# A hybrid encoder block on one core: residual with tokens on the partitions, down and output projections with activations as stationary operand

## The chip, the cores and the metric

The kernel runs on one core of one Trainium2 chip. A core has a matrix engine (TensorE, PE in the profile; PEld is its weight load), a vector engine (VectorE, DVE), a scalar engine (ScalarE, ACT), a general engine (GpSimd, POOL) and an engine that issues transfers (SyncE, SP). TensorE multiplies a stationary operand of up to 128 x 128 with a moving operand of up to 512 columns and adds into PSUM, a memory of eight banks of 512 float32 for each of 128 partitions. The metric is the device time of one execution in microseconds, as the median of the runs.

## The reference

One block of an encoder on 512 tokens of 1024 features, all in float32: a half feed-forward layer, a token mixer of two branches, a second half feed-forward layer, a norm. The projections dominate.

```python
def rms_norm(x, g):
    return x * rsqrt(mean(x * x, axis=-1) + 1e-6) * g

def swiglu_ffn(h, w_gate, w_up, w_down):          # hidden width 2816
    return (silu(h @ w_gate) * (h @ w_up)) @ w_down

x = x + 0.5 * swiglu_ffn(rms_norm(x, ffn1_norm), ffn1_w_gate, ffn1_w_up, ffn1_w_down)
h = rms_norm(x, mix_norm)
u_a, v_a, q_r, k_r, v_r, g_r, gate_a, gate_b = split(h @ w_in + b_in)      # eight times 1024 columns
a = spatial_gating(gelu(u_a), gelu(v_a), ...)                              # 128-position chunks
r = bidirectional_retention(rotary(q), rotary(k) / 16, v, decay)           # four heads of 256
r = r * rsqrt(mean(r * r, per head) + 1e-6) * silu(g_r)
mix = sigmoid(gate_a) * (a @ w_branch_a) + sigmoid(gate_b) * (r @ w_branch_b)
x = x + mix @ w_out
x = x + 0.5 * swiglu_ffn(rms_norm(x, ffn2_norm), ffn2_w_gate, ffn2_w_up, ffn2_w_down)
return rms_norm(x, final_norm)
```

## The kernel before

Every float32 product is made of three matmuls (`mm3`, lines 90 to 93): each operand is split into a part hi that a single pass carries exactly and the rest lo, and hi·hi, hi·lo and lo·hi are added up in PSUM. Weights come in tiles of 1 MB (`load_w`, lines 80 to 88): SyncE loads `raw`, ScalarE copies it to `whi` (line 85), VectorE subtracts to `wlo` (line 87). Each of the three kinds has two buffers. Activations are split in the same way into tiles of the pool `act` with 60 buffers; PSUM is a ring of eight banks.

The residual x lies with features on the partitions: x[m] holds 128 features of all 512 tokens. A projection (`proj`, line 95) has 128 columns of a weight as the stationary operand and 512 tokens as the moving one, and gives features on the partitions again. Only where the mixer wants tokens on the partitions (`tok_block`, the values of both branches) the activations are stationary and 512 columns of the weight move; those products are named pv and pva in the profile.

A norm over features then crosses partitions. `Norm.add` (line 109) squares each x[m] on ScalarE and adds up on VectorE; `Norm.stats` (line 123) sums over the partitions by small matmuls with a column of ones (n_pss), takes the power -0.5 on GpSimd, lays the result on a diagonal in two parts, and `spread` (line 147) multiplies that by ones, so that each partition has the factor of all tokens (n_pbc). The projections behind a norm take h = x times the norm's weight, split by `scaled_split` (line 159), and the factor 1/rms comes in later, when the outputs leave PSUM (`bc`, or `tok` for tokens on the partitions). So the projections need not wait for the norm. n1, n2, n3 and n4 are the norms before feed-forward a, the mixer, feed-forward b and the output.

A feed-forward layer (`ffn`, line 171) makes 11 pairs of 128 hidden features (`gate_up`), and `down` takes them in three chunks of 8, 8 and 6 tiles. After the last chunk of a, `on_x1` (line 288) splits x[m] for the mixer, adds its square to n2 and stores it to `x_dram`; `wo` (lines 606 to 620) reads it back, adds the output projection, and makes h3 and n3. In feed-forward b the last chunk is done by `last` (line 637) in two halves of 256 tokens, so that the first half's norm n4 and its stores lie behind the products of the second.

The order of the instructions on each engine comes from a scheduler, which places them by its own times and respects the pools. Where `tc.manual_schedule` stands, around the start and around `last`, they stand in the order of the code. Each engine carries out its queue in order; an instruction that waits holds up what is behind it.

Of the kernel before, what the change touches and what calls it, by code (L numbers as in the profile page):

```python
# [30 lines left out]
# columns of the per-feature vectors  # L31
C_G1, C_GM, C_G2, C_GF, C_B = 0, 8, 16, 24, 32
C_N = 96
# row vectors, broadcast over the partitions
R_BV, R_BVR, R_SG, R_SB, R_BS, R_DEC = 0, 1024, 2048, 3072, 4096, 4608
R_N = 4616
# [3 lines left out]
def block_kernel(ctx, tc, xT, wg1, wu1, wd1, w_in, wa, wb, wo, wg2, wu2, wd2, cols_d, rows_d, ws_d, cos_d, sin_d, out):  # L40
# [31 lines left out]
    def split(src, name, lo_pool=None):  # L72
        """The two parts of a float32 tile that one TensorE pass carries exactly."""
# [21 lines left out]
    def proj(o, wt, j, acts, first=True, last=True):  # L95
        """o[feature, token] += w[:, j-th 128 columns].T @ acts"""
        whi, wlo = wt
        n = len(acts)
        for k, (hi, lo) in enumerate(acts):
            mm3(o, whi[:, k, j * P:(j + 1) * P], wlo[:, k, j * P:(j + 1) * P], hi, lo,  # L100
                first and k == 0, last and k == n - 1)

    class Norm:
        """Sum of squares of feature-major tiles, and from it the inverse root mean square."""
# [11 lines left out]
        def behind(self):  # L116
            """Order what follows behind the last term of the sum."""
# [5 lines left out]
        def stats(self, n):  # L123
            """Per token, with tokens on the partitions; then on a diagonal, to be spread by `spread`."""
# [22 lines left out]
        def spread(self):  # L147
            """The same along the free axis, on all partitions."""
# [10 lines left out]
    def scaled_split(x, col, name):  # L159
        """Both parts of x * cols[:, col]."""  # L160
# [10 lines left out]
    def ffn(tag, x, h, norm, wg, wu, wd, on_x, first=None, last=None, last_weights=None, aside=None):  # L171
        """x += 0.5 * swiglu(h); h lacks the factor 1 / rms, which norm gives."""
        bc = None
        hidden = {}
        chunks = [(0, 8), (8, 8), (16, 6)]

        def weights(p):
            wgt = load_w(wg, 0, KT, p * 256, 256, f"{tag}g{p}")
            with norm.behind() if p == 0 else ExitStack():
                return wgt, load_w(wu, 0, KT, p * 256, 256, f"{tag}u{p}")  # L180

        def gate_up(p, wt):
            nonlocal bc
            pss = []
            for j in range(2):
                pg = PS(f"{tag}pg")
                proj(pg, wt[0], j, h)
                if bc is None and j == 0:
# [4 lines left out]
                if bc is None:  # L193
# [3 lines left out]
        def evacuate(p, pss):  # L197
            for j, (pg, pu) in enumerate(pss):
                tgt = T(f"{tag}tg")
                nc.vector.tensor_tensor(out=tgt, in0=pg, in1=bc, op=ALU.mult)  # L200
                nc.scalar.activation(tgt, tgt, AF.Silu)
                tut = T(f"{tag}tu")
                nc.vector.tensor_tensor(out=tut, in0=pu, in1=bc, op=ALU.mult)  # L203
                nc.vector.tensor_tensor(out=tut, in0=tut, in1=tgt, op=ALU.mult)
                hidden[2 * p + j] = split(tut, f"{tag}hid")

        def down(c):
            f0, nf = chunks[c]
            acts = [hidden.pop(f0 + i) for i in range(nf)]
            for mp in range(4):  # L210
                wt = load_w(wd, f0, nf, mp * 256, 256, f"{tag}d{c}_{mp}")
                pd = [PS(f"{tag}pd") for _ in range(2)]
                for j in range(2):
                    proj(pd[j], wt, j, acts[:-2], last=False)
                for j in range(2):
                    whi, wlo = wt
                    for i, (hi, lo) in enumerate(acts[-2:]):
                        k = nf - 2 + i
                        mm3(pd[j], whi[:, k, j * P:(j + 1) * P], wlo[:, k, j * P:(j + 1) * P], hi, lo, False, i == 1)
                for j in range(2):  # L220
                    m = 2 * mp + j
                    nc.vector.scalar_tensor_tensor(out=x[m], in0=pd[j], scalar=0.5, in1=x[m], op0=ALU.mult, op1=ALU.add)  # L222
                    if c == len(chunks) - 1:
                        on_x(m)

        p0 = 0
# [530 lines left out]
```

## Time and profile before

| | |
|---|---|
| time, median of 3 runs | 1283.22 us (1282.95 to 1283.3) |
| span of the profiled execution | 1281.6 us |
| TensorE busy | 1270.8 us, 99% of the span |
| VectorE busy | 653.1 us, 51% |
| ScalarE busy | 393.6 us, 31% |
| GpSimd busy | 12.1 us, 1% |
| read from and written to memory | 122.74 MB and 4.19 MB |

The profiled execution's span and the runs' median are 1.6 us apart. Starts in a timeline are from the span's begin. A matmul's record is longer than the distance to the next one's start, since matmuls overlap; the distance between starts is what one of them costs. In a timeline a row with xN stands for N instructions in a row.

### The profile page before, as it was taken

Reading aid. Unit: us, or ns where it says so; the run is one execution under the profiler, and the core shown is the slowest. Engines: PE = TensorE matmul, PEld = TensorE weight load, DVE = VectorE, ACT = ScalarE, POOL = GpSimd, SP = SyncE. Lnnn points to the kernel's source line nnn. Section 1 sums busy time; section 2 is a strip of 40 time slices with the busy share of each in tenths; the row PEclk is TensorE's granted clock in tenths of the full one; section 3 lists DMA queues with packets and bytes.
Section 4 is the critical chain, followed back from the end, with each engine's and each line's share of the span. In section 5 each row is a group of like instructions: output and inputs, shape, how many; then the busy total and the mean of one; then the engine's idle time right before and its main releaser. Section 6 shows DMA issues by size and latency. Waiting matters only on the chain.

```text
span 1281.6 us, 13501 instructions
## 1 busy us (share of the span) xinstructions
PE 1270.8 (99%) x5787; PEld 1056.0 (82%) x5787; DVE 653.1 (51%) x789; ACT 393.6 (31%) x427; POOL 12.1 (1%) x17
## 2 busy tenths in 40 slices
PE   9999999999999999999999999999999999999997
PEld 6888888888888888888888888888888888888897
DVE  6644355534467575675297434345544434353453
ACT  6322124212243232333244222223322212231232
POOL 0000000000000000000000000000000000000000
PEclk9999999999999999999999999999999999999998
DMA  8223313322343223234223333343242322233221
GB/s 283 80 66 131 98 58 108 111 91 87 113 158 99 66 66 99 67 99 131 66 66 99 99 99 99 99 152 112 66 131 66 129 90 91 86 102 96 90 75 66
DMA packets 116155, 127.79 MB, mean 100 GB/s; under 512 B 2944, under 2 KB 106368, under 8 KB 116096
## 3 DMA queue, kind: packets, MB, share of 16 engines
q1 hardware_dynamic: 116096, 126.94, 30.9%
q8 instruction: 45, 0.74, 0.2%
q14 instruction: 14, 0.11, 0.0%
HBM read 122.74 MB, written 4.19 MB: 99 GB/s over the span
## 4 chain that ended last, share of the span: by engine, by line
PE 99%; DMA 0%; DVE 0%; SPq 0%; ACT 0%; POOLq 0%; issue 0%; DVEq 0%; ACTq 0%
PE apg L91 3%; PE bpd L91 3%; PE bpd L93 3%; PE bpd L92 3%; PE apg L92 3%; PE apg L93 3%; PE apu L91 3%; PE apu L92 3%; PE apu L93 3%; PE bpu L91 3%; PE bpu L93 3%; PE bpg L93 3%; PE apd L92 3%; PE bpg L92 3%; PE apd L91 3%; PE bpu L92 3%
## 5 line engine op out<-in xcount | busy, mean ns | idle before, releaser
L91 PE MATMUL bpu<-h_hi,bu_whi 128*128 128x512 f32 x176 | 68.6, 390 | 0.0
L93 PE MATMUL bpu<-h_hi,bu_wlo 128*128 128x512 f32 x176 | 68.5, 389 | 0.0
L93 PE MATMUL bpg<-h_hi,bg_wlo 128*128 128x512 f32 x176 | 68.5, 389 | 0.0
L92 PE MATMUL bpg<-h_lo,bg_whi 128*128 128x512 f32 x176 | 68.5, 389 | 0.0
L91 PE MATMUL bpg<-h_hi,bg_whi 128*128 128x512 f32 x176 | 68.5, 389 | 0.0
L92 PE MATMUL bpu<-h_lo,bu_whi 128*128 128x512 f32 x176 | 68.5, 389 | 0.0
L91 PE MATMUL apd<-ahid_hi,ad_whi 128*128 128x512 f32 x176 | 68.5, 389 | 0.0
L92 PE MATMUL apd<-ahid_lo,ad_whi 128*128 128x512 f32 x176 | 68.5, 389 | 0.0
L93 PE MATMUL apd<-ahid_hi,ad_wlo 128*128 128x512 f32 x176 | 68.5, 389 | 0.0
L91 PE MATMUL apu<-h_hi,au_whi 128*128 128x512 f32 x160 | 62.4, 390 | 0.0
L93 PE MATMUL apu<-h_hi,au_wlo 128*128 128x512 f32 x160 | 62.3, 389 | 0.0
L93 PE MATMUL apg<-h_hi,ag_wlo 128*128 128x512 f32 x160 | 62.3, 389 | 0.0
L92 PE MATMUL apg<-h_lo,ag_whi 128*128 128x512 f32 x160 | 62.3, 389 | 0.0
L91 PE MATMUL apg<-h_hi,ag_whi 128*128 128x512 f32 x160 | 62.2, 389 | 0.0
L92 PE MATMUL apu<-h_lo,au_whi 128*128 128x512 f32 x160 | 62.2, 389 | 0.0
L91 PE MATMUL bpd<-bhid_hi,bd_whi 128*128 128x512 f32 x128 | 49.8, 389 | 0.0
L92 PE MATMUL bpd<-bhid_lo,bd_whi 128*128 128x512 f32 x128 | 49.8, 389 | 0.0
L93 PE MATMUL bpd<-bhid_hi,bd_wlo 128*128 128x512 f32 x128 | 49.8, 389 | 0.0
L222 DVE SCALAR_TENSOR_TENSOR x<-apd,x 128x512 f32<-128x512 f32 x24 | 16.6, 692 | 58.0 <-PE apd L93 58.0
L203 DVE TENSOR_TENSOR btu<-bpu,n_bc 128x512 f32<-128x512 f32 x22 | 15.2, 691 | 59.0 <-PE bpu L93 59.0
L203 DVE TENSOR_TENSOR atu<-apu,n_bc 128x512 f32<-128x512 f32 x22 | 15.2, 689 | 49.2 <-PE apu L93 49.2
L92 PEld LDWEIGHTS bpu<-h_lo,bu_whi 128*128 128x128 f32 x176 | 33.1, 188 | 6.9
(302 smaller groups left out, 3141.2 us busy)
## 6 DMA issues: line engine op xcount, KB each, us to landing
bg_raw<-in_wg SPq DMA_DIRECT2D x11, 1024.0 KB, 5.3
bu_raw<-in_wu SPq DMA_DIRECT2D x11, 1024.0 KB, 5.3
ag_raw<-in_wg SPq DMA_DIRECT2D x10, 1024.0 KB, 5.3
au_raw<-in_wu SPq DMA_DIRECT2D x10, 1024.0 KB, 5.5
ad_raw<-in_wd SPq DMA_DIRECT2D x8, 1024.0 KB, 5.1
bd_raw<-in_wd SPq DMA_DIRECT2D x8, 1024.0 KB, 5.0
q_raw<-in_w_in SPq DMA_DIRECT2D x4, 1024.0 KB, 5.4
k_raw<-in_w_in SPq DMA_DIRECT2D x4, 1024.0 KB, 5.3
```

The costliest lines, as they stand in the source:

```text
L91: nc.tensor.matmul(o, lhi, rhi, start=first, stop=False)
L92: nc.tensor.matmul(o, lhi, rlo, start=False, stop=False)
L93: nc.tensor.matmul(o, llo, rhi, start=False, stop=last)
L203: nc.vector.tensor_tensor(out=tut, in0=pu, in1=bc, op=ALU.mult)
L222: nc.vector.scalar_tensor_tensor(out=x[m], in0=pd[j], scalar=0.5, in1=x[m], op0=ALU.mult, op1=ALU.add)
```

## The change

- The residual has tokens on the partitions: x[j][half] is 128 tokens by 512 features. `down` and the output projection take activations as the stationary operand and 512 columns of the weight as the moving one. The weights of the last down chunk stay resident and are used tile by tile (`last_part`).
- The input of feed-forward a is still read with features on the partitions (`xf`) for its norm and products. The residual is read a second time, with tokens on the partitions, from a second input `xr` (`load_x`), before the first update.
- `TokNorm`: a norm per token, without TensorE. ScalarE squares a tile and sums along its row at once, VectorE adds the halves' sums and the constant, GpSimd takes the power, ScalarE scales (`n_xn`). `turn` brings 128 x 128 pieces of that back to features on the partitions with transposes on TensorE (n_pt), two features' tiles by 256 tokens to a PSUM bank, from where ScalarE makes h_hi and VectorE h_lo, now with the norm's weight and the factor 1/rms both in them.
- `hand_over` is written out by hand and used twice, for n2 at the end of feed-forward a and for n3 at the output projection. It goes by two groups of 256 tokens: the products of three quarters of x, the first group's norm, the loads of the next stage's first weights, the last quarter, the turn of the first group, the second group's norm, the next stage's first four outputs for 256 tokens, and the same for the second group. Those outputs are q and k of head 0, and the first pair of feed-forward b.
- Everything behind n2 and n3 loses the multiplication by `bc` or `tok` when it leaves PSUM.
- The final norm n4 (`end2`) goes by tiles of 128 tokens, with no product on TensorE; the output has tokens on the partitions.

```diff
+    class TokNorm:
+        def add(self, j, half):
+            junk = T(self.name + "_sq")
+            nc.scalar.activation(junk, self.x[j][half], AF.Square, accum_out=self.ss[:, j, half:half + 1])
+        def stats(self, j0, n):
+            ...
+            nc.vector.tensor_tensor(out=var, in0=self.ss[:, js, 0], in1=self.ss[:, js, 1], op=ALU.add)
+            nc.vector.tensor_scalar(out=var, in0=var, scalar1=1.0 / D, scalar2=EPS, op0=ALU.mult, op1=ALU.add)
+            nc.gpsimd.tensor_tensor(out=self.tok[:, js], in0=var, in1=neghalf[:, 0:n], op=ALU.pow)
+        def scale(self, j0, n):
+            for half in range(2):
+                for j in range(j0, j0 + n):
+                    t = T(self.name + "_xn")
+                    nc.scalar.activation(t, self.x[j][half], AF.Copy, scale=self.tok[:, j:j + 1])
+                    self.xn[j, half] = t
+        def turn(self, g, col, h):
+            gs = slice(g * GS, (g + 1) * GS)
+            for mp in range(KT // 2):
+                pt = PS(self.name + "_pt")
+                for i in range(2):
+                    m = 2 * mp + i
+                    for jj in range(GT):
+                        nc.tensor.transpose(pt[:, (i * GT + jj) * P:(i * GT + jj + 1) * P],
+                                            self.xn[g * GT + jj, m // 4][:, (m % 4) * P:(m % 4 + 1) * P], ident)
+                for i in range(2):
+                    ...
+                    nc.scalar.activation(hi[:, gs], src, AF.Copy, scale=gm)
+                    nc.vector.scalar_tensor_tensor(out=lo[:, gs], in0=src, scalar=gm, in1=hi[:, gs].bitcast(F32),
+                                                   op0=ALU.mult, op1=ALU.subtract)
...
+    def hand_over(tag, x, col, h, parts, part, keep):
+        n = TokNorm(tag, x)
+        def block(g, half):
+            for j in range(g * GT, (g + 1) * GT):
+                part(j, half)
+                n.add(j, half)
+                if keep is not None:
+                    nc.sync.dma_start(out=keep[j * P:(j + 1) * P, 512 * half:512 * half + 512], in_=x[j][half])
+        with tc.manual_schedule(engines=ENGINES):
+            block(0, 0)
+            block(1, 0)
+            block(0, 1)
+            n.stats(0, GT)
+            n.scale(0, GT)
+            todo = parts()
+            block(1, 1)
+            n.turn(0, col, h)
+            n.stats(GT, GT)
+            n.scale(GT, GT)
+            for wt, po, j in todo:
+                proj_group(po, wt, j, h, 0)
+            n.turn(1, col, h)
+            for wt, po, j in todo:
+                proj_group(po, wt, j, h, 1)
...
+    def wo_part(j, half):
+        js = slice(j * P, (j + 1) * P)
+        po = PS("po")
+        for kh in range(2):
+            if (half, kh) not in wos:
+                wos[half, kh] = load_w(wo, 4 * kh, 4, 512 * half, 512, f"wo{half}{kh}")
+        for k in range(KT):
+            whi, wlo = wos[half, k // 4]
+            mm3(po, mix[k][0][:, js], mix[k][1][:, js], whi[:, k % 4, :], wlo[:, k % 4, :], k == 0, k == KT - 1)
+        nc.vector.tensor_tensor(out=x[j][half], in0=po, in1=x[j][half], op=ALU.add)
```

**SyncE at the end of feed-forward a.** The rows are the loads and stores that SyncE issues there: q0, k0, pv0 and pv1 are the mixer's first weights, x_dram the store of x (before: x0 to x7 by features; after: x20 is tile 2, first half). Before:

```order
L291 DMA x_dram_95<-x0_87 128x512
L291 DMA x_dram_95<-x1_88 128x512
L82 DMA q0_raw_2460<-in_w_in 128x8x256
L291 DMA x_dram_95<-x2_89 128x512
L291 DMA x_dram_95<-x3_90 128x512
L82 DMA k0_raw_2560<-in_w_in 128x8x256
L291 DMA x_dram_95<-x4_91 128x512
L291 DMA x_dram_95<-x5_92 128x512
```

And of the change:

```order
L455 DMA x_dram_95<-x20_1029 128x512
L455 DMA x_dram_95<-x30_1031 128x512
L455 DMA x_dram_95<-x01_1026 128x512
L455 DMA x_dram_95<-x11_1028 128x512
L82 DMA q0_raw_2443<-in_w_in 128x8x256
L82 DMA k0_raw_2449<-in_w_in 128x8x256
L82 DMA pv0_raw_2834<-in_w_in 128x4x512
L82 DMA pv1_raw_2888<-in_w_in 128x4x512
L455 DMA x_dram_95<-x21_1030 128x512
```

q0 and k0 stood behind the second and the fourth of eight stores and now stand, side by side, behind the sixth.

**ScalarE at the same place.** n2_sq are the squares of the norm, q0_whi and k0_whi the hi parts of the mixer's first weights, h2_hi and n2_h_hi those of the mixer's input. Before:

```order
L163 ACTIVATE h2_hi_2381<-x4_91,cols_75 128x512
L111 ACTIVATE n2_sq_2385<-x4_91 128x512
L85 CAST q0_whi_2462<-q0_raw_2460 128x2048
L163 ACTIVATE h2_hi_2390<-x5_92,cols_75 128x512
L111 ACTIVATE n2_sq_2394<-x5_92 128x512
L163 ACTIVATE h2_hi_2443<-x6_93,cols_75 128x512
L111 ACTIVATE n2_sq_2447<-x6_93 128x512
L163 ACTIVATE h2_hi_2452<-x7_94,cols_75 128x512
L111 ACTIVATE n2_sq_2456<-x7_94 128x512
L85 CAST k0_whi_2562<-k0_raw_2560 128x2048
```

And of the change, here with the engine that each row waits for:

```order
L185 ACTIVATE n2_sq_2424,n2_ss_2285<-x11_1028 128x512 [waits DVE_49,Activation_49]
L198 ACTIVATE n2_xn_2431<-x00_1025,n2_tok_2286 128x512 [waits Activation_49,Pool_49]
L198 ACTIVATE n2_xn_2433<-x10_1027,n2_tok_2286 128x512 [waits Activation_49]
L198 ACTIVATE n2_xn_2435<-x01_1026,n2_tok_2286 128x512 [waits Activation_49]
L198 ACTIVATE n2_xn_2437<-x11_1028,n2_tok_2286 128x512 [waits Activation_49]
L85 CAST q0_whi_2445<-q0_raw_2443 128x2048 [waits DMAHW3_49,PE_49]
L85 CAST k0_whi_2451<-k0_raw_2449 128x2048 [waits DMAHW4_49,PE_49]
L185 ACTIVATE n2_sq_2475,n2_ss_2285<-x21_1030 128x512 [waits DVE_49,Activation_49]
L185 ACTIVATE n2_sq_2498,n2_ss_2285<-x31_1032 128x512 [waits DVE_49,Activation_49]
L218 ACTIVATE n2_h_hi_2506<-n2_pt_2501,cols_75 128x256 [waits PE_49]
L218 ACTIVATE n2_h_hi_2510<-n2_pt_2501,cols_75 128x256 [waits DVE_49]
L218 ACTIVATE n2_h_hi_2519<-n2_pt_2514,cols_75 128x256 [waits PE_49]
```

The mixer's input was made from each x tile as it came, with q0_whi between; now q0_whi and k0_whi stand ahead of the last two squares, and all parts of the mixer's input behind them. Of each two h_hi the first waits for TensorE's transposes and the second for VectorE. On VectorE the order is the same: q0_wlo, k0_wlo, the updates of x21 and x31, then the h_lo.

**ScalarE at the output projection.** wo0 to wo3 are its weight tiles before (256 columns each); wo10 and wo11 are, after, the tiles of the second 512 columns, b00 and b10 the first weights of feed-forward b. Before:

```order
L85 CAST wo1_whi_5839<-wo1_raw_5837 128x2048
L75 CAST mix_hi_5746<-gt_5565 128x512
L111 ACTIVATE n3_sq_5802<-xb0_5750 128x512
L163 ACTIVATE h3_hi_5798<-xb0_5750,cols_75 128x512
L85 CAST wo2_whi_5911<-wo2_raw_5909 128x2048
L163 ACTIVATE h3_hi_5830<-xb1_5752,cols_75 128x512
```

And of the change:

```order
L185 ACTIVATE n3_sq_6004,n3_ss_5906<-x20_5890 128x512
L185 ACTIVATE n3_sq_6032,n3_ss_5906<-x30_5892 128x512
L85 CAST wo10_whi_6037<-wo10_raw_6035 128x2048
L85 CAST wo11_whi_6043<-wo11_raw_6041 128x2048
L185 ACTIVATE n3_sq_6072,n3_ss_5906<-x01_5887 128x512
L185 ACTIVATE n3_sq_6100,n3_ss_5906<-x11_5889 128x512
L198 ACTIVATE n3_xn_6106<-x00_5886,n3_tok_5907 128x512
L198 ACTIVATE n3_xn_6108<-x10_5888,n3_tok_5907 128x512
L198 ACTIVATE n3_xn_6110<-x01_5887,n3_tok_5907 128x512
L198 ACTIVATE n3_xn_6112<-x11_5889,n3_tok_5907 128x512
L85 CAST b00_whi_6116<-b00_raw_6114 128x2048
L85 CAST b10_whi_6122<-b10_raw_6120 128x2048
```

wo2_whi stood behind the work on the first x tile, two weight tiles ahead of its own products; wo10_whi now stands behind the squares of x20 and x30, the tiles made directly before its own products, and b00_whi and b10_whi behind the first group's norm.

## Rows read from the trace of the kernel before

**Rows 1.** Page: busy us of each engine, granted clock by slice, chain by engine.

```profile
PE 1270.8 (99%) x5787; PEld 1056.0 (82%) x5787; DVE 653.1 (51%) x789; ACT 393.6 (31%) x427; POOL 12.1 (1%) x17
...
PEclk9999999999999999999999999999999999999998
...
PE 99%; DMA 0%; DVE 0%; SPq 0%; ACT 0%; POOLq 0%; issue 0%; DVEq 0%; ACTq 0%
```

**Rows 2.** Waits of TensorE: engine, line, releaser: us in total, times, longest.

```profile
PE n_pbc L693 <- DVE n_diag L687: 1.5, 1, 1.5
```

**Rows 3.** Timeline of TensorE: start us, us, engine, line, operation, out<-in.

```profile
399.82 0.39 PE L91 MATMUL pv<-pv_whi,h_hi 128*128 128x512 f32 x1
...
403.90 0.39 PE L91 MATMUL pv<-pv_whi,h_hi 128*128 128x512 f32 x1
...
1257.39 0.28 PE L92 MATMUL bpd<-bhid_lo,last_hi 128*128 128x256 f32 x1
...
1261.46 0.28 PE L93 MATMUL bpd<-bhid_hi,last_lo 128*128 128x256 f32 x1
```

**Rows 4.** Timeline of TensorE, the norm n2 among the q products.

```profile
374.53 0.95 PE L128 MATMUL n_pss<-ones,n_sq 128*128 128x2 f32 x8
...
381.41 0.40 PE L91 MATMUL k<-h_hi,k_whi 128*128 128x512 f32 x1
```

**Rows 5.** Timeline of TensorE: ahead of n4's sums, and the last product.

```profile
1255.81 0.28 PE L93 MATMUL bpd<-bhid_hi,last_lo 128*128 128x256 f32 x1
...
1270.37 0.28 PE L93 MATMUL bpd<-bhid_hi,last_lo 128*128 128x256 f32 x1
```

**Rows 6.** Groups by line and shape: busy us, mean ns, idle before, releasers.

```profile
L111 ACT ACTIVATE n_sq<-x 128x512 f32<-128x512 f32 x16 | 9.3, 619 | 0.1
L672 ACT ACTIVATE n_xg<-xb,cols 128x256 f32<-128x256 f32 x16 | 7.9, 497 | 0.0
L85 ACT CAST q_whi<-q_raw 128x2048 fp32r<-128x2048 f32 x4 | 7.7, 1913 | 5.4 <-PE pv L93 2.7 <-PE k L92 2.7
...
L222 DVE SCALAR_TENSOR_TENSOR x<-apd,x 128x512 f32<-128x512 f32 x24 | 16.6, 692 | 58.0 <-PE apd L93 58.0
L87 DVE TENSOR_TENSOR q_wlo<-q_raw,q_whi 128x2048 fp32r<-128x2048 f32 x4 | 9.2, 2291 | 0.5 <-ACT q_whi L85 0.5
L682 DVE TENSOR_SCALAR n_var<-n_pss 128x2 f32<-128x2 f32 x2 | 0.3, 156 | 1.7 <-PE n_pss L680 1.7
...
L685 POOL TENSOR_TENSOR n_tok<-n_var,neghalf 128x2 f32<-128x2 f32 x2 | 1.4, 696 | 358.0 <-DVE n_var L682 358.0
```

**Rows 7.** Timeline of the tail, the last work on VectorE.

```profile
1275.54 2.48 DVE L696 TENSOR_TENSOR n_xg<-n_xg,n_pbc 128x512 f32<-128x512 f32 x4 [1.31 <-PE n_pbc L693]
```

**Rows 8.** Transfers of 1 MB: page (last column us to landing) and one tile.

```profile
q_raw<-in_w_in SPq DMA_DIRECT2D x4, 1024.0 KB, 5.4
...
DMA to landing us min/median/max: 5.2/5.5/10.3
```

**Rows 9.** Timeline: from ScalarE to VectorE and from VectorE to ScalarE.

```profile
13.11 0.73 ACT L163 ACTIVATE h_hi<-x,cols 128x512 fp32r<-128x512 f32 x1
13.88 0.75 DVE L165 SCALAR_TENSOR_TENSOR h_lo<-x,cols,h_hi 128x512 fp32r<-128x512 f32 x1 [0.15 <-ACT h_hi L163]
...
1255.41 0.42 DVE L662 SCALAR_TENSOR_TENSOR xb<-bpd,xb 128x256 f32<-128x256 f32 x1 [3.17 <-PE bpd L93]
1255.93 0.42 ACT L664 ACTIVATE n_acc<-xb 128x256 f32<-128x256 f32 x1 [2.78 <-DVE xb L662]
```

**Rows 10.** Chain in order of time: start us, us, what; the spatial gating.

```profile
671.04 3.57 PE psg L554 x32
```

**Rows 11.** Windows: busy us (count) by engine, granted clock, DMA share, GB/s.

```profile
1274.20:1275.60 1.40, 1.22 (x2) 0.50 (x2) 0.09 (x2) 0.00 (x0) 0.00 (x0) 0.50 0.00 0
```

**Rows 12.** Timeline of TensorE, among the first products.

```profile
7.09 0.63 PE L92 MATMUL apg<-h_lo,first_hi 128*128 128x512 f32 x1
...
10.08 0.63 PE L93 MATMUL apg<-h_hi,first_lo 128*128 128x512 f32 x1
```

More of the change, by code (lines that the diff above doesn't have):

```diff
@@ L187, in gate_up @@
                 proj(pg, wt[0], j, h)
-                if bc is None and j == 0:
+                if norm is not None and bc is None and j == 0:
                     norm.stats(D)
@@ L192, in gate_up @@
                 pss.append((pg, pu))
-                if bc is None:
+                if norm is not None and bc is None:
                     bc = norm.spread_sb()
@@ L226, in ffn @@
-        p0 = 0
-        if first is not None:
-            with tc.manual_schedule(engines=ENGINES):
-                pss0 = first([(PS(f"{tag}pg"), PS(f"{tag}pu")) for _ in range(2)])
-                wt = weights(1)
-                for k in range(KT):
-                    norm.add(x[k])
-                pss = gate_up(1, wt)
-                for eng in (mybir.EngineType.SP, mybir.EngineType.Activation, mybir.EngineType.DVE):
-                    started.append([i for i in nc.cur_bb.bb.instructions if i.engine == eng][-1])
-            evacuate(0, pss0)
-            evacuate(1, pss)
-            p0 = 2
+            hf = nf // 2
@@ new lines, in last_weights @@
+        def last_weights():
+            f0, nf = CHUNKS[2]
+            w = {}
+            for half in range(2):
+                for k0 in range(0, nf, 3):
+                    raw = wp.tile([P, 3, 512], F32, tag="raw", name="last_raw")
+                    nc.sync.dma_start(
+                        out=raw, in_=wd[(f0 + k0) * P:(f0 + k0 + 3) * P, 512 * half:512 * half + 512].rearrange(
+                            "(k p) c -> p k c", p=P))
+                    for i in range(3):
+                        w[half, k0 + i] = split(raw[:, i, :], "last")
+            return w
@@ L239, in ffn, with last_part @@
+        def last_part(w, acts, j, half):
+            js = slice(j * P, (j + 1) * P)
+            po = PS(f"{tag}pl")
+            nf = len(acts)
+            for k in range(nf):
+                mm3(po, acts[k][0][:, js], acts[k][1][:, js], *w[half, k], k == 0, k == nf - 1)
+            nc.vector.scalar_tensor_tensor(out=x[j][half], in0=po, scalar=0.5, in1=x[j][half], op0=ALU.mult, op1=ALU.add)
+        p0 = first(weights, gate_up, evacuate)
         for p in range(p0, NF // 2):
             wt = weights(p)
-            if last is not None and p == NF // 2 - 1:
-                last_w = last_weights(wd, *chunks[2])
+            if p == NF // 2 - 1:
+                last_w = last_weights()
@@ L293, in block_kernel @@
+    h2 = []
+    x_dram = dram.tile([S, D], F32, name="x_dram")
     hctx = ExitStack()
@@ L587, in block_kernel @@
                 t = T("gt")
[L588 to L589 removed]
+                nc.scalar.activation(t, pg, AF.Sigmoid, bias=bias(off + P * (2 * mp + j)))
                 gates.append(t)
@@ L621, in block_kernel @@
-    del mix
-    lp = ctx.enter_context(tc.tile_pool(name="lp", bufs=6))
-    def last_weights(wd, f0, nf):
-        w = {}
-        for cp in range(2):
-            for k0 in range(0, nf, 3):
-                raw = wp.tile([P, 3, 512], F32, tag="raw", name="last_raw")
-                nc.sync.dma_start(out=raw, in_=wd[(f0 + k0) * P:(f0 + k0 + 3) * P, 512 * cp:512 * cp + 512].rearrange(
-                    "(k p) c -> p k c", p=P))
-                for i in range(3):
-                    w[cp, k0 + i] = split(raw[:, i, :], "last", lp if cp else None)
-        return w
```

361 lines of the change are left out of this document (165 added, 196 removed).

## The prediction

> **What bounds the kernel now.** I read the page's busy table and the shares of the chain first: TensorE is busy for 99% of the span and is 99% of the chain that ended last [rows 1]. The view of waits on TensorE comes next: its largest entry is 1.5 us, in the very end [rows 2]. So the time is a count of matmuls times their spacing, and a change pays only by taking matmuls off TensorE or shortening the ends; whatever makes TensorE wait is added in full. The spacing is read from starts: 18 intervals of 512 columns between the two pv rows give 0.2267 us, 34 intervals of 256 columns between the two bpd rows give 0.1197 [rows 3]. The pv products already have activations as the stationary operand and stand at the same spacing as the others, so turning the operands round in `down` and `wo` costs nothing by itself, and their number stays.
>
> **What the change takes away.**
> - n2 and n3: from n_pss to the first k product there are 6.88 us and 24 products in between, 5.44 us; the rest, 1.44, is the norm's own matmuls [rows 4]. Twice: 2.9.
> - n4's sums between the last halves: 1.58 us from the bpd product before them to the second one behind [rows 3, 5], less two slots of 0.12: 1.3.
> - Last down part: 288 products of 256 columns (34.5 us) become 144 of 512 (32.6): 1.8.
> - The tail: from the last product's start (1270.37) to the span's end is 11.2 us [rows 5]. After the change the last tile needs its product (0.4), an x update of 0.69, a Square of 0.62, two sums of 0.16, a pow of 0.70, two scalings of 0.75 and some 0.3 of handing over [rows 6], 4.5 together; behind the last scaling come the 3.6 us that now lie between the last VectorE end (1275.54 + 2.48) and 1281.6 [rows 7]. 8.1 against 11.2: 3.1.
>
> Sum 9.1. The multiplications by bc that go from VectorE and the hidden tiles' saved steps are worth nothing: TensorE never waits for them today. The second reading of x (2 MB) and the residual's updates lie beside products that wait for nothing else, some 10 us for each tile of outputs (48 x 0.2267), so nothing either; if that cover failed, a late x tile would hold VectorE and then a PSUM bank.
>
> **What it adds.** Two hand-overs, each with the same three waits in a row.
>
> (a) *The weights come late, n2.* Call T0 the end of the products of x01 and x11; behind them TensorE has x21 and x31, 36 products, 8.2 us. SyncE's q_raw and k_raw now stand behind the store of x11, which waits for x11's update (T0 + 0.85). They are issued at about T0 + 1.4 and 1.8. A single transfer lands after 5.4 us; of two issued back to back the later took 10.3 [rows 8]. I take T0 + 6.8 for q and 10 for k (7.1 to 12.1). On ScalarE q_whi and k_whi (1.91 each) stand ahead of the Squares of x21 and x31, and on VectorE q_wlo and k_wlo (2.29 each) ahead of the updates of x21 and x31 [rows 6]; so what came off TensorE at T0 + 8.2 waits for k_raw. k_whi ends at 11.95, k_wlo at 14.3, the two updates at 15.0 and 15.7, the last Square at 16.4, and only then comes the first h_hi of the turn. TensorE has its transposes, then nothing from about T0 + 10 on.
>
> (b) *The two readers of one bank alternate.* The turned features stand two to a PSUM bank; ScalarE writes h_hi, VectorE h_lo, and in the program's order each second h_hi waits for the h_lo of the first. ScalarE's 128x256 with a column takes 0.497 [rows 6], VectorE's 128x256 0.42 [the row at 1255.41, rows 9], for which I take 0.48 because of the column (512 columns take 0.75 with one at 13.88 and 0.69 in the update's row [rows 6, 9]); the passing on is 0.04 from ScalarE to VectorE and 0.10 back [rows 9]. A bank so takes 0.497 + 0.04 + 0.48 + 0.10 + 0.497 less a small overlap, 1.53, and four banks with the last h_lo and the products behind it 7.0 us, in which the first output's 24 products (2.9) lie. Its ends: 4.2 if ScalarE alone sets the pace, 9.7 if each read costs what the 512-wide rows do. I take 7.0, the sum from rows of the same shape. The Trainium skill ("PSUM — Partial Sum Buffer", section "PSUM bank collisions raise a hardware error") says that two engines must not touch one bank at the same time, reads included; it gives the reason for that order, and no run here shows it. By that rule the 4.2 could not be had without another layout of the banks.
>
> (c) *Both token groups do this.* Behind the first output the other three take 72 x 0.1197 = 8.6. Then the second group: four transposes of the first bank (0.9, at the 0.223 of a 128x128 f32 product: 3.57 us for 16 [rows 10]), 7.0, and 8.5: 16.4. The bounds of a transpose are 0.06 (half of a 256-wide slot) and 0.223; the other banks' lie beside ScalarE's work.
>
> n2 from T0: 16.4 + 7.0 + 8.6 + 16.4 = 48.4. Before, the same products took 8.2 + 96 x 0.2267 = 29.9. **+18.4.**
>
> (d) *n3 has more.* At the start of `wo` the second weight tile's lo part comes at 4.35 us (1.91 + 2.29 + handing over) behind the end of the merge, whose buffer it takes, and is asked for at 2.95: +1.45. At the end of x30's product (Te) ScalarE has wo10_whi behind the Square of x30: update until 0.85, Square until 1.57, wo10_whi until 3.5, wo10_wlo until 5.85. TensorE has nothing else, so the next 48 products take 16.55 in place of 10.9. The first FFN b weights then wait for the hi buffers of wo10 and wo11, which the products of x31 free at T0 + 8.2 and T0 + 10.9; b10_whi ends at 12.96, b10_wlo at 15.3, the updates at 16.65, the Square at 17.35. With 7.0 + 8.5 + 16.4 that is 49.3 from T0 and 65.85 from Te, against 2 x 10.88 + 21.76 = 43.5: +22.3. **Together +23.8.**
>
> (e) *The clock.* In the end's stretch, with TensorE hardly fed, the granted clock was 0.50 [rows 11]. The page's row of it is full in every other slice [rows 1], the first too; but the first products stand 0.427 apart (seven intervals, 7.09 to 10.08) against 0.227 later [rows 12], and I read that as the lower level of 1.2 GHz; full spacing comes some ten products later. A fall thus costs up to some ten slots of 0.2, 2 us. The gap at wo10 and the four turns can each fall: 0 to 10 us in all; I take 4 (the wo10 gap whole, the turns a half each).
>
> **Sum.** 1281.6 + 18.4 + 23.8 + 4 - 9.1 = 1318.7 of span. The median of the runs, 1283.2, lies 1.6 above the profiled span, so 1320.3: I forecast 1320, slower by 37. The ends: with 4.2 a turn -11, no fall of the clock -4, q and k 1 us sooner: about 1303; with 9.7 a turn +11, all falls +6, k 2 us later: about 1339.
>
> **Rivals.**
> - *The clock falls at every turn and stays low over it.* For: all four turns are transposes and waits; against: the idle rows of before are few. With two slots of products at 0.427 lost in each, about 1.5 us more per turn: 1320 + 6 = 1326. The Trainium skill ("TensorE: Matmul & The Clock Gate", section "Part 4: PE-mode transpose") says that transposes do not count as busy for the clock; no run here shows it yet. Chance 0.13.
> - *The turn overlaps better than (b).* ScalarE runs ahead into the next bank while VectorE is in the last: four banks come at ScalarE's pace, 4.2 in place of 7.0: 1320 - 11 = 1309. For: other banks are there; against: each engine has them in one fixed order. Chance 0.12.
> - *Not slower: the weights are not late.* Place: q_raw, k_raw and the wo and FFN b weights. If these have landed and are split when TensorE comes (which decides: k_wlo and the updates by T0 + 9 in place of 15.7, wo10_wlo by Te), all waits of (a) and (d) go, and with overlapped turns only the transposes and the narrow products remain: 64 x 0.06 = 3.8, plus 2 x 96 x 2 x 0.1197 less 2 x 96 x 0.2267 = 2.4, together 6.2 against 9.1 saved: 1280 to 1282, the same or faster. For: SyncE has time in front of the stage; against: its queue is in order, and the ring of two buffers for raw, hi and lo leaves no place ahead. Chance 0.05.
> - *The gaps are halves.* The late weights cost as in (a) and (d), but one of two (k_raw landing at once, or wo10) is not late: 1308 to 1314. Part of the forecast's own range.
>
> Forecast 0.70, with a range of its own of 1308 to 1332. From these cases 80% lie between 1302 and 1334. What a measurement of this kernel can tell from no change is 0.2%, 2.6 us. Faster by more than that 0.03, within it 0.02, slower 0.95.
>
> **What the profile after would show.** TensorE's share falls from 99% to about 95-96%, with some 40 us in the waits, which name h_hi (ScalarE) and h_lo (VectorE) at the turns and wo10 and the first FFN b weights. At the end of FFN a a gap of 5 to 7 us ahead of the first narrow q product; then q outputs of 256 columns in steps with ScalarE's h_hi, about 1.5 us for two features. At `wo` a gap of some 5 us ahead of x01. The granted clock drops below 1.00 in those slices. The tail from the last product to the end is about 8 us. I am wrong if k_raw lands and is split before T0 + 9, if h_hi and h_lo stand beside one another in time, or if the middle of `down` shows waits for x.

## The result

The changed kernel takes 1315.4 us (median of 4 runs, 1314.1 to 1316.8) against 1283.2 before: ratio 1.0253, 95% interval 1.0239 to 1.0268, slower by 32 us. Forecast were 1320 and slower by 37, with 1302 to 1334 as the range. Its profiled span is 1313.2 us, 31.6 more than before.

The page of the changed kernel, the same three lines as in [rows 1]:

```profile
PE 1282.9 (98%) x5851; PEld 1065.3 (81%) x5851; DVE 579.9 (44%) x691; ACT 399.5 (30%) x465; POOL 14.0 (1%) x21
...
PEclk9999999999989999999999999998899999999999
...
PE 92%; DVE 2%; DMA 2%; ACT 2%; issue 1%; SPq 0%; DVEq 0%; POOLq 0%; POOL 0%; ACTq 0%
```

VectorE has lost 73 us of work and it shows nowhere in the time. The chain, 99% TensorE before, now has 6% of VectorE, transfers and ScalarE, and the clock dips in two places. The waits of TensorE name both, where before the longest was 1.5 us [rows 2]:

```profile
PE q L91 <- ACT n_h_hi L218: 7.5, 1, 7.5
PE bpg L91 <- ACT n_h_hi L218: 5.0, 1, 5.0
PE po L91 <- ACT wo_whi L85: 3.4, 1, 3.4
PE po L92 <- DVE wo_wlo L87: 3.0, 2, 1.8
```

Where the time went, from the starts of the same products in both traces:

| first product of | before | after | later by | in this stage | forecast |
|---|---|---|---|---|---|
| feed-forward a, `down` | 118.9 | 117.4 | -1.4 | -1.4 | 0 |
| pv (behind n2, q0 and k0) | 392.3 | 407.8 | 15.5 | +16.9 | +18.0 |
| po | 863.0 | 878.0 | 15.0 | -0.5 | 0 |
| feed-forward b, `down` | 1016.9 | 1055.8 | 38.9 | +23.9 | +25.4 |
| end of the span | 1281.6 | 1313.2 | 31.6 | -7.3 | -6.2 |

The forecast column is the prediction's terms sorted by stage: n2 18.4 + 1 of clock - 1.4; n3 23.8 + 3 of clock - 1.4; the end 1.3 + 1.8 + 3.1. The first row is not the change's doing (see "What was not forecast" below).

The listed waits make up only about half of the loss: all that the view lists come to 22.0 us after and 4.6 before, 17 more. Another 12 lie in the four turns, where the first output's 24 products take 5.6 to 6.2 us in place of 2.9 (24 x 0.1197); between them there are many short waits, their records grow longer (0.38 to 0.58 us for 0.28), and the page counts them as busy.

**The hand-over n2.** T0, the end of the products of x01 and x11, is 36 spacings ahead of the first transposes: 367.67 - 8.16 = 359.51. ScalarE's timeline from there:

```profile
362.44 2.56 ACT L198 ACTIVATE n_xn<-x,n_tok 128x512 f32<-128x512 f32 x4 [1.22 <-POOL n_tok L192]
367.69 1.90 ACT L85 CAST q_whi<-q_raw 128x2048 fp32r<-128x2048 f32 x1 [2.68 <-DMA q_raw<-in_w_in]
370.45 1.90 ACT L85 CAST k_whi<-k_raw 128x2048 fp32r<-128x2048 f32 x1 [0.86 <-DMA k_raw<-in_w_in]
375.37 0.63 ACT L185 ACTIVATE n_sq<-x 128x512 f32<-128x512 f32 x1 [3.02 <-DVE x L311]
...
376.61 0.45 ACT L218 ACTIVATE n_h_hi<-n_pt,cols 128x256 fp32r<-128x256 f32 x1
377.61 0.84 ACT L218 ACTIVATE n_h_hi<-n_pt,cols 128x256 fp32r<-128x256 f32 x2 [0.55 <-DVE n_h_lo L219]
379.04 0.84 ACT L218 ACTIVATE n_h_hi<-n_pt,cols 128x256 fp32r<-128x256 f32 x2 [0.58 <-DVE n_h_lo L219]
```

It waits for q_raw, then for k_raw, then 3.0 us for VectorE's update of x21, which stands behind k_wlo; the first h_hi comes at T0 + 17.1 (forecast 16.4). From there each pair takes 1.42 us, with the 0.55 to 0.58 of waiting for h_lo in it. TensorE in the same stretch:

```profile
367.67 1.91 PE L209 MATMUL n_pt<-ident,n_xn 128*128 128x128 f32 x16
...
377.12 0.58 PE L91 MATMUL q<-n_h_hi,q_whi 128*128 128x256 f32 x1 [7.54 <-ACT n_h_hi L218]
...
383.14 0.28 PE L93 MATMUL q<-n_h_hi,q_wlo 128*128 128x256 f32 x1
...
391.89 1.91 PE L209 MATMUL n_pt<-ident,n_xn 128*128 128x128 f32 x16
...
399.08 0.28 PE L93 MATMUL q<-n_h_hi,q_wlo 128*128 128x256 f32 x1
...
407.83 0.40 PE L91 MATMUL pv<-pv_whi,n_h_hi 128*128 128x512 f32 x1
```

The rows at 383.14 and 399.08 are the 24th products of the first output: it ends 6.65 us behind the first h_hi of its turn (376.61) in the first group and 6.68 (392.52) in the second. 16 transposes take 1.91 with the last one's own 0.27, so 0.109 each.

**The output projection.** TensorE around the last product of x30 and the first of x01:

```profile
901.06 0.39 PE L93 MATMUL po<-wo_whi,mix_lo 128*128 128x512 f32 x1
904.83 0.54 PE L91 MATMUL po<-wo_whi,mix_hi 128*128 128x512 f32 x1 [3.38 <-ACT wo_whi L85]
907.16 0.79 PE L92 MATMUL po<-wo_wlo,mix_hi 128*128 128x512 f32 x1 [1.79 <-DVE wo_wlo L87]
...
911.59 0.58 PE L93 MATMUL po<-wo_whi,mix_lo 128*128 128x512 f32 x1
912.01 0.40 PE L91 MATMUL po<-wo_whi,mix_hi 128*128 128x512 f32 x1
```

Both waits are there, and between 907.7 and 912.0 the products stand 0.427 apart. The windows of that gap and of the turn behind it show the granted clock (before the last two numbers):

```profile
907.10:912.00 4.90, 4.84 (x11) 3.80 (x12) 2.21 (x2) 0.00 (x0) 0.00 (x0) 0.50 0.80 248
...
931.00:933.00 2.00, 1.99 (x18) 1.67 (x15) 2.00 (x1) 1.68 (x1) 0.00 (x0) 1.00 0.00 0
933.00:938.00 5.00, 0.01 (x1) 0.01 (x1) 3.63 (x5) 1.92 (x6) 0.00 (x0) 0.79 0.76 251
938.00:943.00 5.00, 5.00 (x20) 4.40 (x21) 3.08 (x7) 2.77 (x7) 0.00 (x0) 0.53 0.54 170
```

The clock is full over the transposes (931 to 933) and falls over the empty stretch behind them.

**The tail**, to be read against [rows 5, 7]:

```profile
1305.79 0.39 PE L93 MATMUL bpl<-last_hi,bhid_lo 128*128 128x512 f32 x1
1306.21 0.69 DVE L311 SCALAR_TENSOR_TENSOR x<-bpl,x 128x512 f32<-128x512 f32 x1 [3.39 <-PE bpl L93]
...
1308.76 1.41 DVE L765 SCALAR_TENSOR_TENSOR y<-x,n_tok,gf 128x512 f32<-128x512 f32 x2 [0.66 <-POOL n_tok L192]
```

From the last product's start to the end of the span: 7.4 us, where there were 11.2. Gone too is n_pbc of n4's first half, which stood, before, among the products of the second half:

```profile
1261.58 0.59 PE L693 MATMUL n_pbc<-n_diag,ones 128*128 128x256 f32 x2
```

From the bpd product ahead of it (1261.46) to the second one behind (1262.13) it is 0.67 us, less two slots of 0.12: 0.4.

### The profile page after: what moved, and what is told of

Read it like the earlier page. It is cut to its first block, busy times and chain, and to the rows that moved or that the text cites. A ratio compares the mean times of both kernels' runs of the same rounds, so it can differ in the third digit from the quotient of the medians.

```text
span 1313.2 us, 13592 instructions
## 1 busy us (share of the span) xinstructions
PE 1282.9 (98%) x5851; PEld 1065.3 (81%) x5851; DVE 579.9 (44%) x691; ACT 399.5 (30%) x465; POOL 14.0 (1%) x21
## 4 chain that ended last, share of the span: by engine, by line
PE 92%; DVE 2%; DMA 2%; ACT 2%; issue 1%; SPq 0%; DVEq 0%; POOLq 0%; POOL 0%; ACTq 0%
PE bpu L93 3%; PE bpu L91 3%; PE bpu L92 3%; PE bpg L92 3%; PE bpg L93 3%; PE bpg L91 3%; PE apu L91 3%; PE apu L93 3%; PE apu L92 3%; PE apg L93 3%; PE apg L92 3%; PE apg L91 3%; PE pgt L93 2%; PE bpd L93 2%; PE apd L93 2%; PE apd L92 2%
## 5 line engine op out<-in xcount | busy, mean ns | idle before, releaser
L91 PE MATMUL bpg<-n_h_hi,bg_whi 128*128 128x512 f32 x160 | 62.3, 389 | 0.0
L92 PE MATMUL bpg<-n_h_lo,bg_whi 128*128 128x512 f32 x160 | 62.3, 389 | 0.0
L93 PE MATMUL bpg<-n_h_hi,bg_wlo 128*128 128x512 f32 x160 | 62.2, 389 | 0.0
L91 PE MATMUL bpu<-n_h_hi,bu_whi 128*128 128x512 f32 x160 | 62.2, 389 | 0.0
L92 PE MATMUL bpu<-n_h_lo,bu_whi 128*128 128x512 f32 x160 | 62.2, 389 | 0.0
L93 PE MATMUL bpu<-n_h_hi,bu_wlo 128*128 128x512 f32 x160 | 62.2, 389 | 0.0
L91 PE MATMUL apd<-ad_whi,ahid_hi 128*128 128x512 f32 x128 | 49.8, 389 | 0.0
L92 PE MATMUL apd<-ad_wlo,ahid_hi 128*128 128x512 f32 x128 | 49.8, 389 | 0.0
L93 PE MATMUL apd<-ad_whi,ahid_lo 128*128 128x512 f32 x128 | 49.8, 389 | 0.0
L91 PE MATMUL bpd<-bd_whi,bhid_hi 128*128 128x512 f32 x128 | 49.8, 389 | 0.0
```

The source lines that it names most:

```text
L91: nc.tensor.matmul(o, lhi, rhi, start=first, stop=False)
L92: nc.tensor.matmul(o, lhi, rlo, start=False, stop=False)
L93: nc.tensor.matmul(o, llo, rhi, start=False, stop=last)
```

## The experiments

**Only the transfers of q0 and k0 earlier.**

```diff
             block(0, 0)
+            raws["q"], raws["k"] = load_raw(... OFF_Q ...), load_raw(... OFF_K ...)
             block(1, 0)
             block(0, 1)
...
-                wt = load_w(w_in, 0, KT, off, 256, nm + "0")
+                wt = load_w(w_in, 0, KT, off, 256, nm + "0", raws[nm])
```

> Only the two transfers q_raw and k_raw are issued earlier, behind the first two tiles of the hand-over n2; their splits stand where they stood. My theory has two parts in the gap of 7.5 us ahead of the first narrow q product: the late transfers, and the order on ScalarE and VectorE, where q_whi, k_whi, q_wlo and k_wlo stand ahead of the updates and Squares of x21 and x31. With the data there, q_whi starts when the four n_xn are done (T0 + 5.5), k_wlo ends at T0 + 12, the updates follow, the first h_hi comes at about T0 + 14.2 in place of T0 + 17.1: 2.9 us less, about 1312.5. Rival: the place of the transfers is the whole cause, then the gap closes and the time is some 7 us less, about 1308. Rival: the transfers would land in time anyway and only the order counts: no change.

1312.2 us, 3.2 less than the changed kernel. TensorE's wait at this place:

```profile
PE q L96 <- ACT n_h_hi L223: 4.2, 1, 4.2
```

7.5 has become 4.2: the transfers are the smaller part of the gap, and the order on ScalarE and VectorE holds the rest.

**Transfers and splits earlier.**

```diff
             block(0, 0)
+            todo = parts()
             block(1, 0)
             block(0, 1)
             n.stats(0, GT)
             n.scale(0, GT)
-            todo = parts()
             block(1, 1)
```

(for n2 alone.)

> Transfers and splits of q0 and k0 both stand behind the first two tiles of the hand-over n2. By my theory nothing then lies ahead of the updates of x21 and x31: the first h_hi comes at T0 + 9.9 in place of T0 + 17.1, 7.2 us less, about 1308. TensorE's wait there falls from 7.5 to about 0.5 us. Rival (the late transfers are the smaller part, the turn itself keeps TensorE waiting): 3 us or less.

1307.6 us, 7.8 less; the wait for n_h_hi of n2 is almost gone:

```profile
PE q L91 <- ACT n_h_hi L218: 0.2, 1, 0.2
```

With the run before, the gap is accounted for: 3 us to the late transfers, 4 to 5 to the splits that stood ahead of the updates of x21 and x31.

**The output projection's second weights earlier.**

```diff
             mm3(po, ...)
+        if half == 0 and j == NT - 1:
+            for kh in range(2):
+                wos[1, kh] = load_w(wo, 4 * kh, 4, 512, 512, f"wo1{kh}")
         nc.vector.tensor_tensor(out=x[j][half], in0=po, in1=x[j][half], op=ALU.add)
```

> The loads and splits of wo10 and wo11 stand ahead of the update and the Square of x30. By my theory the waits of 3.4 and 1.8 us at the first products of x01 shrink to about 1.4, since wo10 can only be split when the products of x30 let go of the buffers of wo00, and with the short wait the clock does not fall, which now costs 2.0 us over ten products: 6.6 us less, about 1309. If the clock falls all the same: 4.6 less, 1311. Rival: the b0 weights set the end of this stage and the gain is given back at the turn: no change.

1309.3 us, 6.1 less. The trace has one wait of 1.4 us in place of 3.4 and 1.8 (the other of the two in this row is the 1.2 us at the start of the output projection, which the changed kernel has too):

```profile
PE po L92 <- DVE wo_wlo L87: 2.6, 2, 1.4
```

The products behind it are at full spacing: the short gap did not make the clock fall.

**Two banks in turns.**

```diff
-                for i in range(2):
-                    m = 2 * mp + i
+                for m in (m0, m0 + 2, m0 + 1, m0 + 3):       # banks 0, 1, 0, 1
...
-        for k, (hi, lo) in enumerate(acts):
+        for k in (0, 2, 1, 3, 4, 6, 5, 7):
```

> The turned features stay two to a bank, but ScalarE and VectorE take them from two banks in turns (0, 2, 1, 3), so that no h_hi waits for the h_lo before it in its own bank; the products take the features in the same order. By my theory (alternation sets the pace of a turn: 6.7 us from the first h_hi to the end of the first output) a turn takes about 5.0, where the clock is low 5.6, and the four turns give back 5.4 us: about 1310. Rival: TensorE's products, at half the clock behind the gap, set the pace: 0 to 2 us less.

1308.5 us, 6.9 less. The timeline of the second turn of n2 has ScalarE without a pause, six h_hi in a row:

```profile
391.33 2.67 ACT L219 ACTIVATE n_h_hi<-n_pt,cols 128x256 fp32r<-128x256 f32 x6 [7.08 <-PE n_pt L212]
```

Its first output ends 4.66 us behind the first h_hi (6.68 before), and 5.65 (6.65) in the first turn, where the clock is low and TensorE's own products set the pace: 24 at about 0.21. In n3's first turn the first output takes 4.8 us from its first product (934.05 to 938.86) where it took 6.15 (937.99 to 944.14). In n3's second turn it ends 4.66 us behind the first h_hi (948.14 to 952.80) where it ended 6.67 behind (953.41 to 960.08). That is 2.0, 1.0, 1.3 and 2.0, together 6.3 of the 6.9. So alternation in one bank was the pace, and the rival held only for the rest in the two turns at the low clock.

**The three together** (the edits of the last three).

> The three edits of before together: weights of q0 and k0 ahead, wo10 and wo11 ahead, features taken from two banks in turns. If the three act on separate waits, as I hold, their gains add up: 7.8 + 6.2 + 6.9 from 1315.4, so about 1294.5; the low clock behind the gap of n2 goes too, which may give 1 us more. Rival: they share a wait (the gain of the turn lies in the gap that the early weights close), then 1298 or more.

1294.75 us: the gains add up, the three waits are separate.

**The clock by itself.**

```diff
         if half == 1 and j == 0:
+            for _ in range(24):
+                nc.tensor.matmul(po, mix[0][0][:, js], mix[0][0], start=True, stop=True)
...
             n.turn(0, col, h)
+            for _ in range(30 if keep is not None else 20):
+                nc.tensor.matmul(todo[0][1], wh[:, 0, 0:P], wh[:, 0:2, :]..., start=True, stop=True)
```

> The changed kernel with products whose result is thrown away in the three longest gaps: 24 ahead of the first product of x01, 30 behind the first turn of n2, 20 behind that of n3, so that TensorE works on while it would wait. It tells what the fallen clock costs by itself. My reading of the trace: 2.0 us at wo10 (ten products at 0.427), nothing at the two turns, where the alternation of ScalarE and VectorE is slower than the products even at half the clock: about 1313.4. Rival: it costs at all three, 24 narrow products at 0.21 in place of 0.12 in each turn: 6.4 less, 1309. Rival: the products that fill the gaps overrun them: no gain or slower.

1313.0 us, 2.4 less. The starts of the stages tell where: from the first product of feed-forward a's `down` to the first pv it is 290.4 us in both kernels, so nothing came of the filled gap at n2; from the first po to the first product of feed-forward b's `down` it is 175.6 in place of 177.8. A fallen clock cost about 2 us at wo10 and next to nothing at the turns, since at half the clock the products were still about as fast as the alternation that fed them.

**Every wait behind other products.** The steps of the two hand-overs, as lists; a pair is a tile of x, N and V the sums of the two groups, S the second group's scaling, T the first group's turn, 0 and 1 the next stage's weights:

```diff
+        # n2
+        [(0, 0), (1, 0), 0, (0, 1), 1, (1, 1), "N", (2, 0), (3, 0), "T", (2, 1), (3, 1), "V", "S"]
+        # n3, with one more pair of buffers for wo00 and wo11
+        [(0, 0), (1, 0), (2, 0), (3, 0), (0, 1), 0, (1, 1), "N", (2, 1), "T", (3, 1), "V", 1, "S"]
+        # behind either: outputs 1 and 2 of group 0, turn(1), outputs 3 and 4 of group 0, the outputs of group 1
```

> Same residual, same turns and same products as the changed kernel, but every wait of the two hand-overs is put behind other products: weights of q0 and k0 early, one more buffer pair for the output projection's weights, the first group's turn ahead of the last products of x, the second group's turn between the second and the third output of the first group, banks in turns. If the waits are the whole of the loss, what stays is TensorE's own work against the kernel before: 64 transposes at 0.109 (7.0 us) and the narrow outputs (2.4), less the matmuls of n2 and n3 (2.9) and the end that is 7.3 shorter: 1283.2 - 0.8 and about 1 us of rests, 1283 to 1285. Rival: the turned residual costs more than its waits, by the fallen clock at transposes or by contention: 1290 or more.

1294.4 us, a miss by 10. TensorE has a single wait in the hand-overs:

```profile
PE n_pt L215 <- ACT n_xn L201: 10.0, 1, 10.0
```

All of n3 is covered. In n2 I had made the very mistake of the changed kernel: the loads of q0 and k0 stood between the stores of x00, x10 and x01 on SyncE, so each split waited for a transfer that waited for an update, and the next update waited for that split. ScalarE's two splits with their waits:

```profile
350.36 1.91 ACT L88 CAST q_whi<-q_raw 128x2048 fp32r<-128x2048 f32 x1 [5.68 <-DMA q_raw<-in_w_in]
...
361.83 1.90 ACT L88 CAST k_whi<-k_raw 128x2048 fp32r<-128x2048 f32 x1 [5.82 <-DMA k_raw<-in_w_in]
```

**The same with each transpose done twice.**

```diff
-                    for jj in range(GT):
+                    for jj in (0, 0, 1, 1):
```

> The kernel with the covered waits, with each of the 64 transposes done twice. If a transpose costs TensorE its spacing in the trace, 0.109 us: 7.0 slower than the covered kernel. Rival by the Trainium skill (TensorE: Matmul & The Clock Gate, Part 4: PE-mode transpose), that transposes do not count as busy for the clock: the clock falls behind each doubled turn of 3.5 us, and it is slower by 11 or more. Rival: the transposes lie beside ScalarE's reading anyway: no more than 2 slower.

1301.4 us, 7.0 more than the covered kernel: a transpose on the path costs its spacing, no more. At n3, where both turns run at the full clock, the stage is 3.5 us longer, 32 x 0.109. A stretch of 32 in the trace:

```profile
389.60 3.65 PE L215 MATMUL n_pt<-ident,n_xn 128*128 128x128 f32 x32
```

The first turn of n2 in the same trace tests the rival by the rule on transposes directly. It stands behind a wait of 10.4 us, in which the clock fell; the windows of its first part and of what follows, with the granted clock before the last two numbers:

```profile
369.72 6.09 PE L215 MATMUL n_pt<-ident,n_xn 128*128 128x128 f32 x32 [10.41 <-ACT n_xn L201]
```

```profile
369.72:374.40 4.68, 4.68 (x21) 4.36 (x22) 0.76 (x2) 4.15 (x10) 0.00 (x0) 0.50 0.80 297
374.50:375.50 1.00, 1.00 (x11) 1.00 (x10) 0.85 (x3) 0.84 (x2) 0.00 (x0) 1.00 0.00 0
```

TensorE came out of an empty stretch at half the clock and did nothing but transposes, and the clock rose while it did them.

**The covered kernel mended.**

```diff
+        # n2: 2 and 3 issue the transfers of q0 and k0, 0 and 1 split them
+        [2, 3, (0, 0), (1, 0), 0, (0, 1), 1, (1, 1), "N", (2, 0), (3, 0), "T", (2, 1), (3, 1), "V", "S"]
```

> The covered kernel with one thing mended that its trace showed: its single wait on TensorE, 10.0 us for the n_xn of n2, came from q_raw and k_raw, which I had issued between the stores of x00, x10 and x01, so that each split held the next update of x. Now both transfers are issued ahead of the first store, and the splits stay behind x10 and x01. If that wait is the whole of the miss: 10 us less, 1284.5, the sum worked out for the covered kernel (1283 to 1285). Rival: what the turned residual costs beside its waits shows only now: 1288 or more.

1281.6 us (1281.2 to 1282.9, 11 runs), ratio to before 0.9994, interval 0.9985 to 1.0003: no difference that can be told. TensorE waits only at the start:

```profile
PE warm L361 <- DVE warm L356: 1.3, 1, 1.3
PE apg L97 <- ACT first_hi L75: 1.0, 1, 1.0
```

It is 12.8 us less than the covered kernel, 2.8 more than the wait that was removed. Behind that wait the clock had fallen (it read 0.50 until 374.0, where the turn began at 369.47); how much of the 2.8 that is was not measured by itself. With its waits gone the turned residual comes out even, and the whole loss was the waits, those within the turns included; the table below has what is left at each stage.

**The kernel before with the end of the change alone.** x stays with features on the partitions until feed-forward b's second down part is in it, is turned once, and the last part, n4 and the stores are those of the changed kernel.

```diff
+    def turn_x():
+        for j in range(NT):
+            for half in range(2):
+                pt = PS("xpt")
+                for i in range(4):
+                    nc.tensor.transpose(pt[:, i * P:(i + 1) * P], x[4 * half + i][:, j * P:(j + 1) * P], ident)
+                t = A(f"xt{j}{half}", F32)
+                nc.scalar.copy(t, pt)
+                xt[j][half] = t
```

> The kernel before with only the end of the change: x stays with features on the partitions through both feed-forwards and the output projection, is turned once behind the second part of feed-forward b's down projection (32 transposes, evacuated by ScalarE), and the last part of the down projection, n4 and the stores go by tiles of tokens as in the changed kernel. By my theory the end is worth 7.3 us and 32 transposes cost 3.5: 1279.4, faster than both kernels. Rival: the transposes and their copies hide nothing and the last weights or the buffers are late in this order: 1283 or more. Rival: the gain at the end belongs to the whole change and not to the end: no change.

1278.0 us, ratio 0.9966, interval 0.9954 to 0.9979: the fastest of all, 5 us below the kernel before by the medians. Not all of that is the end's. The stages, from the starts of the same products, each less that of the kernel before:

| stage | changed | covered, mended | end alone |
|---|---|---|---|
| up to feed-forward a's `down` | -1.4 | -1.8 | -1.9 |
| to pv (n2) | +16.9 | +3.3 | -0.1 |
| to po | -0.5 | -0.4 | -0.2 |
| to feed-forward b's `down` (n3) | +23.9 | +4.0 | -0.1 |
| to the end of the span | -7.3 | -7.3 | -3.5 |
| span | +31.6 | -2.2 | -5.7 |

The first row is the start, which the end alone does not touch. The end alone is worth 3.5 us, about the 3.8 that were expected (7.3 less 3.5), and the mended covered kernel pays 7.3 us at the two hand-overs for the 7.3 that it gains at the end. The transposes of the end alone in its timeline, and the windows of them and of what follows:

```profile
1210.50 3.65 PE L648 MATMUL xpt<-ident,xb 128*128 128x128 f32 x32
```

```profile
1210.50:1214.10 3.60, 3.60 (x34) 3.60 (x33) 3.02 (x3) 3.59 (x5) 0.00 (x0) 1.00 0.65 218
1214.10:1216.00 1.90, 1.90 (x10) 1.58 (x9) 1.25 (x2) 1.90 (x5) 0.00 (x0) 1.00 0.09 3
```

TensorE does nothing but transposes for 3.6 us, the clock stays at 1.00, and the products behind are at full spacing.

## Why the prediction was right

- *What bounds the kernel.* Right: taking 73 us from VectorE gave nothing, and each wait put ahead of TensorE was paid in full. The runs that removed one wait at a time moved the time by that wait, and by the low clock behind it where there was one.
- *(a) late weights at n2.* Right in order and size: q_raw was there at T0 + 8.2 against 6.8 and k_raw at T0 + 10.9 against 10, so that the first h_hi came at T0 + 17.1 against 16.4, and the runs that moved the transfers and then the splits gave 3.2 and 7.8 us.
- *(b) alternation.* Right as a mechanism, its price a little high: 1.42 us a bank for 1.53, 6.65 a turn for 7.0. The rival that ScalarE would run ahead fell, and the two banks in turns came near what it described, 4.66 us for 4.2. The sentence that this needs another layout of the banks was too strong: another order over the same banks was enough to come near.
- *(c) two groups.* The transposes were priced at 0.223, as 3.57 us for 16 products; but the row has 32 of them [rows 10], which is 0.112 each, and the transposes cost 0.109. Little hung on this misreading. From T0 to the first pv product it is 48.3 us, where the sum said 48.4: the later first h_hi and the cheaper turns and transposes cancel, so that this close agreement is partly luck. (The sum's difference to the 29.9 us before is 18.5, not 18.4.)
- *(d) n3.* T0 there is 920.20 (931.08 less 48 spacings) and Te, the end of x30's product, 901.29, so these products took 18.9 us, 8.0 more than without a wait; forecast were 5.7 and 2.0 of clock. The first h_hi came at T0 + 17.3, forecast 17.4. The wait at the start of the output projection was 1.2 us, forecast 1.45 (by its own terms 4.35 less 2.95, which is 1.40).
- *(e) the clock.* The mechanism was right at wo10, the size wrong at the turns. The 4 us are 2 at wo10 and half a us at each of four turns; the words "a half each" at 2 us for a fall would have made 6. It fell at two turns, behind empty stretches and not over transposes, and cost next to nothing there, since the alternation hid it. The filled gaps gave 2.4 us in all, not 4. The rival with a fall at every turn put 1.5 us on each, for which its two slots of 0.427, 0.85 together, do not account.
- *The Trainium skill's rule on transposes* ("TensorE: Matmul & The Clock Gate", section "Part 4: PE-mode transpose", that they do not count as busy): the runs here speak against it. With the transposes doubled the clock rose from 0.50 to 1.00 while TensorE did nothing else, and doubling them cost 7.0 us, their own spacing. That the clock read 1.00 over 3.6 us of nothing but transposes would not decide it alone, since it also read 1.00 over the empty stretch from 901.5 to 904.5 us in the changed kernel.
- *The savings.* The end gave 7.3 against 6.2: the tail 3.8 rather than 3.1, because 3.0 us and not 3.6 lie behind the last scaling (1308.76 + 1.41 to 1313.2), scaling takes 0.70 and not 0.75 and the power over one column 0.54 and not 0.70. The other 0.4 is the first half's n_pbc, which the sum left out.
- *What was not forecast.* 1.4 us at the start, where this profiled run had the first products at full spacing and that of before did not [rows 12]. It is not the change's doing: the other eleven traces, that of the end alone among them, have their first `down` product at 116.6 to 117.5 us, and only that of the kernel before has it at 118.9. The 15 runs of the kernel before that were made beside the last two experiments lie at 1281.3 to 1281.8 and at 1282.9 to 1283.5, which such a start would explain; no trace shows it for the lower group. The medians of kernels can differ by a part of these 1.6 us for this alone.
- *What the profile would show.* The waits and their places came as forecast in the main, but TensorE's share fell to 98% and not to 95 or 96, and the listed waits are 22 us and not 40: the turns' 12 us lie inside the products' records.
- *The rival on the other side* needed the weights ready and the turns covered, and gave 1280 to 1282. The changed kernel isn't that, but the mended covered one is: 1281.6. That it lands inside is partly luck: the hand-overs cost 7.3 us for its 3.3 (6.2 less 2.9), transposes at 0.109 and not 0.06 above all, and the end gave 7.3 for 6.2, and the early start helped.

The 5.5 us between the forecast's span and the measured one are, but for rounding, the differences of the five stages in the first table: 1.4, 1.1, 0.5, 1.5 and 1.1. All have the same sign, so the total was not hit by errors of two stages that cancel.

## What to carry to other kernels

When one engine is busy for 99% and all others have room, work moved off the others is worth nothing, and a new dependence at a stage's border is worth all it makes that engine wait: follow each in-order queue (the transfers', ScalarE's, VectorE's) through the border and ask what stands ahead of the instruction that TensorE will wait for. A weight load that is hidden in the middle of a stage must be issued and split before the border, ahead of the stores and updates that the border itself waits for. And try the parts of a large change one by one: here the end alone, with half of the transposes, was worth 3.5 us, while the whole was 32 us slower.

## What the runs showed of the hardware that I had not expected

- A transpose of 128x128 f32 costs TensorE 0.109 us in a row of them, about as much as an ordinary f32 product of that shape (3.57 us for 32, [rows 10]).
- Transposes alone brought the granted clock back from 0.50 to 1.00 (the kernel with each transpose done twice, 369.72 to 375.50).
- A Square that also sums its row is followed by an instruction of its own that reads the sum, with a record of 0.19 us.
- A fall of the clock cost nothing where what fed TensorE was slower than its products at half the clock: at n2's first turn six products at 0.21 take some 1.3 us and their two features came every 1.42, and filling the gap ahead of it left the stage at 290.4 us.
